# Value products in two runs of five key tiles, convolution taps spread evenly, a query projection one unit later

## The chip, the cores and the metric

One kernel runs on one core of a Trainium2 chip. The metric is the time of one execution on the device, in microseconds (us). The core has five engines, each with a queue of instructions of its own that it works through in order: TensorE (PE; its weight loads are listed as PEld), VectorE (DVE), ScalarE (ACT), GpSimd (POOL), and SyncE (SP), which here issues the transfers between memory and the on-chip buffers. Engines wait for each other only where data or a buffer makes them.

## The reference

Two layers of a hybrid block work on 1024 latent tokens and 256 context tokens. In each layer one input projection feeds three groups: attention, a convolution and a recurrent group. Their outputs are concatenated and go through one output projection, a normalisation and an MLP.

```python
q_l, k_l, v_l = mla_project(cq, ckv, kr, g_qn, w_uq, g_kvn, w_ukv, True)
q_c, k_c, v_c = mla_project(ccq, cckv, ckr, g_qn, w_uq, g_kvn, w_ukv, False)
att = merge_heads(blocked_attend(q_l, concat([k_l, k_c], 2), concat([v_l, v_c], 2)))
conv = conformer_conv(conv_in, conv_w, conv_b, conv_ln_g, conv_ln_b)   # 31 taps, LayerNorm, swish
h_l, h_c = mlstm_bidirectional(...)
y = concat([att, conv, ml], -1) @ w_out
x = layer_norm(ALPHA * x + g1 * y, ln1_g, ln1_b)
```

`attend` is softmax(q k / sqrt(96)) v over 8 heads. Context tokens attend to context tokens only, and are dropped after the first layer.

## The kernel before, in words

The change touches the attention stage, the method `attention`. The stage works through units: one unit is one head and 128 queries against all 1280 keys, which are 10 key tiles of 128. A group `G` is a pair of heads `p` and a block `g` of 256 queries; it has four units (two heads, two query tiles). There are four pairs. In layer 0 a pair has four groups of latent queries and a small one of context queries, whose two units are mixed into those of the fourth (18 units a pair, 72 in all); in the last layer it has four groups (16 units a pair, 64 in all).

The loop over `i` at the end of the method writes out one unit a turn: the score products of unit `i` (`sc`, L77 to L79), the transposes of unit `i - 2` (`et_ps`, copied by ScalarE to `et`), the softmax of unit `i` (L921 on VectorE, L922 on ScalarE), and then what the table `plan` holds for `i`. The table is filled by `at(i, ...)`: `f` is a group's first unit, `qproj(G, e)` makes the queries of its head `e`, `values(G, j0, j1, fin)` multiplies the key tiles `j0` to `j1` of both heads with the values (L868, tile `pv`), and with the last run `norm` follows (two transposes of the softmax sums, L880, two VectorE steps, and a `spill`). A `pv` product uses 64 of TensorE's 128 output columns: head 0 writes partitions 0 to 63, head 1 partitions 64 to 127.

The convolution hides in the same loop. The 31 taps are steps in the list `taps`: half of the channels on VectorE (L444), half on GpSimd (L449, L450). In a unit that stands in `tap_at`, from unit 2 on, one tap is taken. When `taps` is empty, each further unit takes one step of `post`: three empty ones, a transpose `fwd` for each two token tiles, `norm`, three empty ones, and two steps `back` for each two token tiles. That makes 22 steps in layer 0 (10 token tiles) and 19 in the last layer (8). A `back` step is two transposes (L480, `cb_ps`), two activations (L482, L483, `c_v`), a VectorE step (L484) and a `spill`. What is left of `post` runs after the loop:

```python
            if i < nu:
                if i >= 2 and taps:
                    if i in tap_at:
                        taps.pop(0)(pace[i - 1][:2])
                elif not taps and post:
                    post.pop(0)()
        assert not plan
        while post:
            post.pop(0)()
```

`spill` splits a block into a high and a low part on GpSimd (L86, L92, tile `sp`, one buffer for each of the two pools that it is called with) and stores both with SyncE to `cat_d` in memory, from where the output projection reads its input (`xs_hi`, `xs_lo`, L1187).

After the stage its pools are released, that of the convolution (`cv`) and of the query weights (`wq`) among them. `out_proj` then takes pools in the freed space and loads the eight blocks of the output weights (L1195): blocks 0 to 2 through one buffer `wo_raw`, blocks 3 to 7 into `rw`. VectorE splits each (L87, L92) into two tiles `wo`. The products `y_ps` of the first three token tiles run over the blocks in order, 8 blocks x 3 tiles x 2 halves x 3 products.

Pools and dependencies are tracked by a framework, and a scheduler decides in which order the instructions stand in each engine's queue. It starts from the order of the code, and moves instructions by its own estimate of when they can go.

Of the kernel before, what the change touches and what calls it, by code (L numbers as in the profile page):

```python
# [45 lines left out]
class Kern:  # L46
# [752 lines left out]
    def attention(self, l, last, psc, ps, X, wq, A1, A, B, wqk0, taps, post):  # L799
# [26 lines left out]
        def load(p):  # L826
            wr = wq.tile([P, 640], F32, name="wqk_raw", tag="raw", bufs=1)
            t = [wq.tile([P, 640], F32R, name="wqk_s", tag="wqs", bufs=4) for _ in range(2)]
            wqk[p] = self.load_qk(l, p, wr, t)

        def kproj(p, gi):
            wh, wl = wqk[p]
            t0, n = GROUPS[gi]
            pk = ps.tile([P, 512], F32, name="k_ps", tag="aux")[:, :n]
            c = slice(t0, t0 + n)
            ins = self.mm3(pk, wh[:, 512:640], wl[:, 512:640], self.ckn[0][:, c], self.ckn[1][:, c], True, True)
            for e in range(2):
                kh, kl = kb[(2 * p + e) % 3]
                r = slice(64 * e, 64 * e + 64)
                nc.scalar.copy(kh[0:64, c], pk[r])  # L840
                self.last_lo = nc.vector.tensor_tensor(kl[0:64, c], pk[r], kh[0:64, c].bitcast(F32), ALU.subtract)
            return ins

        def qproj(G, e):
            p, g = groups[G]
            wh, wl = wqk[p]
            t0 = g * 256
            pq = ps.tile([P, 256], F32, name="q_ps", tag="aux")
            for j in range(2):
                c = slice(256 * j + 128 * e, 256 * j + 128 * e + 128)  # L850
                self.mm3(pq, wh[:, c], wl[:, c], self.cqn[0][:, j, t0:t0 + 256], self.cqn[1][:, j, t0:t0 + 256], j == 0, j == 1)
            qf = A.tile([P, 256], F32, name="qf", tag="qf")
            nc.vector.tensor_tensor(qf, pq, self.ropeT[:, t0:t0 + 256], ALU.mult)
            qh, ql = qb[(2 * G + e) % 4]
            self.split(qh, ql, qf, "act", "dve")
            qs[G, e] = (qh, ql)

        def pvmm(G, i):
            p, g = groups[G]
            nk = 10 if g < 4 else 2  # L860
            if i >= nk:
                return
            if i == 0:
                pvs[G] = ps.tile([P, 2, 256], F32, name="pv", tag="pv")
            kt = i if last or g not in (2, 4) else (8 + i) % 10
            for e in range(2):
                h = 2 * p + e
                nc.tensor.matmul(pvs[G][64 * e:64 * e + 64, 0], self.V[:, kt, h * 64:h * 64 + 64], ets[G, e][:, kt],  # L868
                                 start=(i == 0), stop=(i == nk - 1))

        def denom(G):

            nc.vector.reciprocal(nms[G][:, 1], nms[G][:, 1])
            nc.scalar.copy(rbs[G].rearrange("p q e d -> p (q e) d"), nms[G][:, 1][:, :, None].to_broadcast([P, 4, 64]))

        def norm(G):
            p, g = groups[G]
            pr = pvs[G][:, 1]
            for q in range(2):
                nc.tensor.transpose(pr[:, q * P:(q + 1) * P], rbs[G][:, q].rearrange("p e d -> p (e d)"), self.ident)  # L880
            rsb = B.tile([P, 256], F32, name="rsb", tag="rsb", bufs=1)
            nc.vector.tensor_copy(rsb, pr)
            nc.vector.tensor_tensor(rsb, pvs[G][:, 0], rsb, ALU.mult)
            self.spill(A1, p, 2 * g, rsb)
# [69 lines left out]
        units, plan, tap_at = [], {}, set()  # L954

        def at(i, *acts):
            plan.setdefault(i, []).extend(acts)

        def values(G, j0, j1, fin):
            for j in range(j0, j1):  # L960
                pvmm(G, j)
            if fin:
                norm(G)

        for G, (p, g) in enumerate(groups):
            if g == 4:
                continue
            f = len(units)
            if G:
                at(f - 3, lambda G=G: qproj(G, 0))  # L970
                at(f - 2, lambda G=G: qproj(G, 1))
            if g < 3 or last:
                units += [(G, *x) for x in four]
                tap_at |= {f, f + 1, f + 2}
                at(f + 6, lambda G=G: denom(G))
                for k, (j0, j1) in enumerate(((0, 3), (3, 5), (5, 8), (8, 10))):
                    at(f + 6 + k, lambda G=G, j0=j0, j1=j1: values(G, j0, j1, j1 == 10))
            else:
                units += [(G, 0, 0), (G, 0, 1), (G + 1, 0, None), (G, 1, 0), (G, 1, 1), (G + 1, 1, None)]
                tap_at |= {f, f + 1, f + 3, f + 4}  # L980
                at(f - 1, lambda G=G: qproj(G + 1, 0))
                at(f + 2, lambda G=G: qproj(G + 1, 1))
                at(f + 6, lambda G=G: denom(G))
                at(f + 7, lambda G=G: values(G, 0, 10, True))
                at(f + 8, lambda G=G: denom(G + 1))
                at(f + 9, lambda G=G: values(G + 1, 0, 2, True))
            if g == 0 and p + 1 < HEADS // 2:
                at(f, lambda p=p: load(p + 1))
            if g == 3 and p + 1 < HEADS // 2:
                for gi, k in enumerate((2, 2, 3) if last else (3, 4, 5)):  # L990
                    at(f + k, lambda p=p, gi=gi: kproj(p + 1, gi))
# [1297 lines left out]
```

## Time and profile before

| what | value |
|---|---|
| three runs | 3201.37, 3201.81, 3207.8 us; median 3201.81 us |
| the profiled execution | 3209.91 us, its span 3208.1 us |
| TensorE busy, share of the span | 3050.6 us, 95% |
| VectorE, ScalarE, GpSimd busy | 2069.2, 1391.5, 1314.7 us (64%, 43%, 41%) |
| attention stage, first to last value product | layer 0: 387.9 to about 730 us; layer 1: to 2376.8 us |

The profile is of one execution. Busy time is the union of an engine's instructions; matmuls overlap in the array, and an instruction's own time is longer than the distance to the next. An idle time is put down to what ended it.

### The profile page before, as it was taken

Reading aid. Unit: us, or ns where it says so; the run is one execution under the profiler, and the core shown is the slowest. Engines: PE = TensorE matmul, PEld = TensorE weight load, DVE = VectorE, ACT = ScalarE, POOL = GpSimd, SP = SyncE. Lnnn points to the kernel's source line nnn. Section 1 sums busy time; section 2 is a strip of 40 time slices with the busy share of each in tenths; the row PEclk is TensorE's granted clock in tenths of the full one; section 3 lists DMA queues with packets and bytes.
Section 4 is the critical chain, followed back from the end, with each engine's and each line's share of the span. In section 5 each row is a group of like instructions: output and inputs, shape, how many; then the busy total and the mean of one; then the engine's idle time right before and its main releaser. Section 6 shows DMA issues by size and latency. Waiting matters only on the chain. (4 is left out here: it accounts for less than half of the span.)

```text
span 3208.1 us, 50116 instructions
## 1 busy us (share of the span) xinstructions
PE 3050.6 (95%) x19354; PEld 2542.6 (79%) x19354; DVE 2069.2 (64%) x3562; ACT 1391.5 (43%) x2736; POOL 1314.7 (41%) x1134
## 2 busy tenths in 40 slices
PE   7999999999899999999999999999999899999987
PEld 4779777777699999777777879777767899977765
DVE  3164678655854444778898265677648755578897
ACT  2142566672443333433334332566644433353332
POOL 0021488210321111477771531477111422268885
PEclk9999999999999999999999999999999899999998
DMA  7521100026433333544423432100053333342322
GB/s 261 199 67 49 47 18 15 16 72 233 166 121 105 106 105 108 168 157 133 157 87 134 159 81 59 47 14 14 15 202 132 105 104 104 105 145 98 103 95 99
DMA packets 213583, 337.23 MB, mean 105 GB/s; under 512 B 13760, under 2 KB 134592, under 8 KB 211296
## 3 DMA queue, kind: packets, MB, share of 16 engines
q1 hardware_dynamic: 213344, 334.03, 32.0%
q8 instruction: 152, 2.49, 0.3%
q14 instruction: 87, 0.71, 0.1%
HBM read 253.05 MB, written 80.92 MB: 104 GB/s over the span
## 5 line engine op out<-in xcount | busy, mean ns | idle before, releaser
L1379 PE MATMUL c_ps<-xs_hi,wm 128*128 128x256 f32 x2560 | 512.4, 288 | 12.7 <-DVE rw L2185 9.5
L1379 PEld LDWEIGHTS c_ps<-xs_hi,wm 128*128 128x128 f32 x2560 | 422.3, 195 | 21.7 <-DVE rw L2185 10.0
L1379 PE MATMUL o_ps<-xs_hi,xs_lo 128*128 128x512 f32 x1458 | 379.3, 398 | 27.3 <-DVE acc L2185 20.3
L1379 PE MATMUL c_ps<-xs_lo,wm 128*128 128x256 f32 x1280 | 366.8, 287 | 3.2 <-DVE xs_lo L2185 3.2
L1379 PEld LDWEIGHTS o_ps<-xs_hi,xs_lo 128*128 128x128 f32 x1458 | 271.9, 190 | 97.9 <-DVE acc L2185 25.9
L2185 DVE TENSOR_TENSOR acc<-o_ps,acc 128x512 f32<-128x512 f32 x405 | 270.9, 682 | 63.1 <-PE o_ps L1379 61.8
L1379 PEld LDWEIGHTS c_ps<-xs_lo,wm 128*128 128x128 f32 x1280 | 249.5, 195 | 3.9 <-DVE xs_lo L2185 3.6
L84 ACT COPY et<-et_ps 128x512 f32<-128x512 f32 (+1 forms) x392 | 198.7, 515 | 95.5 <-PE et_ps L947 90.5
L1379 PE MATMUL c_ps<-bx,wm 128*128 128x256 f32 x1536 | 230.3, 289 | 4.1 <-ACT bx L2185 2.3
L1379 PEld LDWEIGHTS c_ps<-bx,wm 128*128 128x128 f32 x1536 | 206.6, 196 | 7.5 <-POOL bx L2185 3.0
L1379 PE MATMUL o_ps<-wm,xs_lo 128*128 128x512 f32 x783 | 206.8, 396 | 5.3 <-DVE acc L2185 5.3
L92 DVE TENSOR_TENSOR wm<-rw,wm 128x512 fp32r<-128x512 f32 x175 | 140.1, 802 | 109.8 <-ACT wm L84 104.7
L84 ACT CAST wm<-rw 128x512 fp32r<-128x512 f32 x175 | 108.4, 621 | 229.9 <-PE c_ps L1379 175.1
L1409 POOL TENSOR_TENSOR w_s<-w_s,rw 128x512 f32<-128x512 f32 x30 | 40.3, 1343 | 380.8 <-DVE wm L92 380.8
L868 PE MATMUL pv<-et,V 128*64 128x256 f32 x1312 | 194.6, 391 | 0.0
L1379 PEld LDWEIGHTS o_ps<-wm,xs_lo 128*128 128x128 f32 x783 | 146.3, 189 | 40.7 <-DVE acc L2185 7.2
L450 POOL TENSOR_TENSOR conv_acc<-conv_acc,tap 128x656 f32<-128x656 f32 x120 | 170.4, 1420 | 9.7
L921 DVE TENSOR_SCALAR_CACHE_REDUCE E<-sc 128x1280 f32<-128x1280 f32 x91 | 135.5, 1489 | 60.2 <-PE sc L79 59.4
L1443 ACT ACTIVATE hb<-c_ps,fm 128x256 f32<-128x256 f32 x240 | 112.7, 474 | 129.3 <-PE c_ps L1379 119.9
L77 PE MATMUL sc<-kq 128*128 128x512 f32 (+1 forms) x400 | 166.0, 415 | 2.1 <-DVE E L921 1.2
L2185 POOL TENSOR_TENSOR xs_hi<-rw,xs_hi 128x512 fp32r<-128x512 f32 x94 | 138.8, 1492 | 57.2 <-ACT xs_hi L2185 56.7
L947 PE MATMUL et_ps<-ident,E 128*128 128x128 f32 x910 | 149.4, 276 | 1.8 <-ACT et L84 1.2
(504 smaller groups left out, 7785.3 us busy)
## 6 DMA issues: line engine op xcount, KB each, us to landing
rw<-in_w_mlp SPq DMA_DIRECT2D x126, 512.0 KB
hb<-h_d SPq DMA_DIRECT2D x72, 512.0 KB
h_d<-hb SPq DMA_DIRECT2D x64, 512.0 KB
wada<-in_w_ada SPq DMA_DIRECT2D x96, 256.0 KB
cat_d<-sp SPq DMA_DIRECT2D x144, 128.0 KB
wada<-in_w_ada SPq DMA_DIRECT2D x16, 1024.0 KB
w_raw<-in_w_in SPq DMA_DIRECT2D x20, 512.0 KB
xs_hi<-cat_d SPq DMA_DIRECT2D x18, 512.0 KB
```

Source lines behind the costliest of these rows:

```text
L77: mm(ps, lh, rh, start=first, stop=False)
L84: return nc.scalar.copy(out, in_)
L92: return h, e.tensor_tensor(lo, src, hi.bitcast(F32), ALU.subtract)
L450: nc.gpsimd.tensor_tensor(aj[:, c], aj[:, c], m, ALU.add)
L868: nc.tensor.matmul(pvs[G][64 * e:64 * e + 64, 0], self.V[:, kt, h * 64:h * 64 + 64], ets[G, e][:, kt], start=(i == 0), stop=(i == nk - 1))
L921: dve = nc.vector.tensor_scalar(E, s[:, c], -1.0, None, ALU.mult, ALU.min, accum_out=nms[G][:, 0, x:x + 1])
L947: nc.tensor.transpose(pt[:, j], E[:, (i0 + j) * P:(i0 + j + 1) * P], self.ident)
L1379: ins = self.nc.tensor.matmul(ps, x, y, start=first and i == 0, stop=i == len(todo) - 1, skip_group_check=True)
L1409: tt(sums[i], sums[i], a11, ALU.subtract)
L1443: self.nc.scalar.activation(h[:, :, q], b, AF.Identity, bias=f[:, FM_B1 + 2 * i + q % 2:FM_B1 + 2 * i + q % 2 + 1])
L2185: ins = f(*a, **k)
```

## The change

The value products of a group of four units come in two runs of five key tiles, at its units `f + 6` and `f + 8`, and no longer in four runs of three, two, three and two at `f + 6` to `f + 9`. The second query projection of a group comes one unit before the group's first, and no longer two. And where a group took a tap in three of its four units, it now takes one in every other; only the first group of each pair in layer 0, and the first three of each pair in the last layer, keep three.

```diff
             f = len(units)
             if G:
                 at(f - 3, lambda G=G: qproj(G, 0))
-                at(f - 2, lambda G=G: qproj(G, 1))
+                at(f - 1, lambda G=G: qproj(G, 1))
             if g < 3 or last:
                 units += [(G, *x) for x in four]
-                tap_at |= {f, f + 1, f + 2}
+
+                tap_at |= {f, f + 1, f + 2} if g < (3 if last else 1) else {f, f + 2}
                 at(f + 6, lambda G=G: denom(G))
-                for k, (j0, j1) in enumerate(((0, 3), (3, 5), (5, 8), (8, 10))):
-                    at(f + 6 + k, lambda G=G, j0=j0, j1=j1: values(G, j0, j1, j1 == 10))
+                for k, j0, j1 in (6, 0, 5), (8, 5, 10):
+                    at(f + k, lambda G=G, j0=j0, j1=j1: values(G, j0, j1, j1 == 10))
```

The scheduler makes more of it than the diff tells, in the two attention stages and up to the start of the output projections. Three places follow. First, TensorE in layer 0, a run of value products of before; `et_ps` are the transposes of softmax rows, `sc` the scores.

```order
L79 MATMUL sc<-kq 128x256
L947 MATMUL et_ps<-ident,E_3276 128x128 x2
L868 MATMUL pv<-et,V 64x256 x6
L947 MATMUL et_ps<-ident,E_3277 128x128
L77 MATMUL sc<-kq 128x512
```

And such a place in the changed kernel:

```order
L79 MATMUL sc<-kq 128x256
L868 MATMUL pv<-et,V 64x256
L947 MATMUL et_ps<-ident,E_3276 128x128 x2
L868 MATMUL pv<-et,V 64x256 x9
L880 MATMUL pv<-ident,rb 128x128 x2
```

Where three key tiles of both heads stood in one run, five now stand in two: one product alone, then two transposes, then nine. Over both layers there were 172 runs, 72 of them of an odd number of products; now there are 152, 124 of them odd, with 656 products in either.

Second, TensorE where the attention stage of layer 0 ends, before:

```order
L947 MATMUL et_ps<-ident,E_3277 128x128 x10
L868 MATMUL pv<-et,V 64x256
L935 MATMUL et_ps<-ident,krT 128x128 x4
L868 MATMUL pv<-et,V 64x256 x19
L880 MATMUL pv<-ident,rb 128x128 x2
L77 MATMUL y_ps<-wo_6824,xs_hi 128x512
L78 MATMUL y_ps<-wo_6825,xs_hi 128x512
```

The same place after:

```order
L868 MATMUL pv<-et,V 64x256 x15
L880 MATMUL pv<-ident,rb 128x128 x2
L480 MATMUL cb_ps<-ident,zt 128x128 x6
L868 MATMUL pv<-et,V 64x256 x4
L880 MATMUL pv<-ident,rb 128x128 x2
L77 MATMUL y_ps<-wo_6824,xs_hi 128x512 x2
L78 MATMUL y_ps<-wo_6825,xs_hi 128x512
```

Three `back` steps (`cb_ps`, two transposes each) now stand behind the long run of value products. In the last layer two of them stand there, behind a run of twenty.

Third, SyncE at the same place, before (`wo_raw` and `rw` are loads of output weights, `xs_hi` and `xs_lo` of the projection's input, `cat_d` the stores of a spill):

```order
L504 DMA cat_d_96<-sp 128x2x128
L1195 DMA wo_raw<-in_w_out 128x1024 x2
L1187 DMA xs_hi<-cat_d_95 128x1024 x2
L1195 DMA wo_raw<-in_w_out 128x1024
L504 DMA cat_d_95<-sp 128x2x128
L504 DMA cat_d_96<-sp 128x2x128
L1187 DMA xs_hi<-cat_d_95 128x1024 x3
L504 DMA cat_d_95<-sp 128x2x128
```

and after:

```order
L504 DMA cat_d_95<-sp 128x2x128
L504 DMA cat_d_96<-sp 128x2x128
L1188 DMA xs_lo<-cat_d_96 128x1024
L1196 DMA rw<-in_w_out 128x1024
L1196 DMA wo_raw<-in_w_out 128x1024
L1196 DMA rw<-in_w_out 128x1024 x3
L1196 DMA wo_raw<-in_w_out 128x1024
L1196 DMA rw<-in_w_out 128x1024
```

Before, three pairs of stores still came behind the first weight load; now the first weight load stands behind the last of all stores. It is the same in the last layer.

## Rows read from the trace of the kernel before

**Rows 1.** Busy by stretch: us, length, busy PE, PEld, DVE, ACT, POOL (instructions), PEclk, DMA.

```profile
400.00:725.00 325.00, 323.12 (x2152) 238.06 (x2152) 227.26 (x379) 221.00 (x438) 181.23 (x169) 1.00 0.11 33
2075.00:2375.00 300.00, 299.24 (x2003) 220.72 (x2004) 194.16 (x312) 205.65 (x382) 148.55 (x158) 1.00 0.10 32
```

**Rows 2.** Timeline of TensorE in layer 0: start us, us, what, [idle <- what ended it].

```profile
460.81 0.65 PE L868 MATMUL pv<-et,V 128*64 128x256 f32 x4
461.39 0.20 PEld L947 LDWEIGHTS et_ps<-ident,E 128*128 128x128 f32 x2 [0.38 <-issue]
...
705.66 0.65 PE L868 MATMUL pv<-et,V 128*64 128x256 f32 x2
706.23 0.44 PE L947 MATMUL et_ps<-ident,E 128*128 128x128 f32 x2
706.60 1.51 PE L868 MATMUL pv<-et,V 128*64 128x256 f32 x10
708.04 0.39 PE L77 MATMUL q_ps<-cqn,wqk_s 128*128 128x256 f32 x1
...
720.53 1.04 PE L947 MATMUL et_ps<-ident,E 128*128 128x128 f32 x8
```

**Rows 3.** Timeline: a `back` step of layer 0, its first activation and its split.

```profile
655.50 0.56 ACT L482 ACTIVATE c_v<-cb_ps,fm 128x256 f32<-128x256 f32 x1 [0.58 <-PE cb_ps L480]
...
657.56 0.73 POOL L92 TENSOR_TENSOR sp<-c_v,sp 128x256 fp32r<-128x256 f32 x1
```

**Rows 4.** Timeline of GpSimd at the end of layer 0's attention.

```profile
729.38 0.41 POOL L86 TENSOR_SCALAR sp<-rsb 128x256 fp32r<-128x256 f32 x1 [6.32 <-DVE rsb L883]
...
732.64 0.41 POOL L86 TENSOR_SCALAR sp<-rsb 128x256 fp32r<-128x256 f32 x1 [2.04 <-DMA cat_d<-sp]
```

**Rows 5.** Timelines: first weight loads of layer 0, and layer 1's with their splits.

```profile
709.04 6.14 SPq L1195 DMA_DIRECT2D wo_raw<-in_w_out  x2
...
2359.50 0.73 POOL L92 TENSOR_TENSOR sp<-c_v,sp 128x256 fp32r<-128x256 f32 x1
2362.77 0.35 SPq L1195 DMA_DIRECT2D wo_raw<-in_w_out  x1
2366.71 0.69 DVE L87 CAST wo<-wo_raw 128x1024 fp32r<-128x1024 f32 x1 [2.00 <-DMA wo_raw<-in_w_out]
2367.44 1.23 DVE L92 TENSOR_TENSOR wo<-wo_raw,wo 128x1024 fp32r<-128x1024 f32 x1
2368.69 0.33 SPq L1195 DMA_DIRECT2D wo_raw<-in_w_out  x1
```

**Rows 6.** Timelines: normaliser's transposes, and first use of the three tiles, either layer.

```profile
727.80 0.44 PE L880 MATMUL pv<-ident,rb 128*128 128x128 f32 x2
763.42 2.05 DVE L1248 TENSOR_TENSOR rw<-y_ps,g 128x512 f32<-128x512 f32 x3 [7.10 <-PE y_ps L79]
...
2377.09 0.44 PE L880 MATMUL pv<-ident,rb 128*128 128x128 f32 x2
2412.24 2.05 DVE L1248 TENSOR_TENSOR rw<-y_ps,g 128x512 f32<-128x512 f32 x3 [10.80 <-PE y_ps L79]
```

**Rows 7.** Timelines: the five later weights of layer 0, issued and first used.

```profile
737.15 2.96 SPq L1195 DMA_DIRECT2D rw<-in_w_out  x5
743.03 0.69 DVE L87 CAST wo<-rw 128x1024 fp32r<-128x1024 f32 x1 [11.23 <-DMA rw<-in_w_out]
```

**Rows 8.** Timeline of TensorE in layer 0's output projection, behind a wait.

```profile
734.96 0.72 PE L79 MATMUL y_ps<-wo,xs_lo 128*128 128x512 f32 x2 [1.89 <-DMA xs_lo<-cat_d]
...
735.99 0.63 PE L79 MATMUL y_ps<-wo,xs_lo 128*128 128x512 f32 x1
...
738.55 0.63 PE L77 MATMUL y_ps<-wo,xs_hi 128*128 128x512 f32 x1
...
741.46 0.39 PE L77 MATMUL y_ps<-wo,xs_hi 128*128 128x512 f32 x1
741.69 0.39 PE L78 MATMUL y_ps<-wo,xs_hi 128*128 128x512 f32 x1
```

## The prediction

> **What bounds the kernel now.** I read the busy time by stretch first, because the change touches only the two attention stages and the place where each hands over to the output projection. Over most of both stages TensorE is busy 323.12 of 325 us and 299.24 of 300 us at full granted clock, while VectorE, ScalarE and GpSimd are busy at most 70% of the time [rows 1]. So inside attention a TensorE microsecond is a microsecond of the kernel, and work moved on the other engines costs nothing while it stays under that cover. The reader is to see there that only 1.88 + 0.76 = 2.6 us of visible TensorE idle time are left to win. Next I read TensorE's timeline for the price of the value products (`pv`), and then the timelines of ScalarE, GpSimd, SyncE and VectorE around the ends of the stages, because the order of the changed kernel moves transfers there.
>
> **Value products.** Two `pv` records are one product of one head. A run of one product lasts 0.57 us until the next instruction starts (705.66 to 706.23), a run of two 0.58 us (460.81 to 461.39), a run of five 1.44 us (706.60 to 708.04) [rows 2]. From run two to run five are two more pairs, (1.44 - 0.58) / 2 = 0.43 us each. The two heads of a key tile write different halves of the output partitions, and a pair takes what a single one takes: an odd run wastes half a pair. Beside its pairs a run costs 0.58 - 0.43 = 0.15 us when it is left (the next weights wait 0.38 us for no other engine), and at its start the two transposes ahead of it hold TensorE 0.37 us, where two in a long series take 2 x 1.04 / 8 = 0.26 us [rows 2]: 0.11 us, together 0.26 us a run.
>
> Counting the order, before has 172 runs of `pv`, 72 of them odd, which makes (656 + 72) / 2 = 364 pairs; after has 152 runs, 124 odd, 390 pairs. The four runs of 6, 4, 6, 4 that the code asks for mostly stood whole; the two runs of ten mostly become one and nine, since the scheduler lets the first product go ahead of two late transposes. So 26 pairs x 0.43 = +11.2 us, and 20 runs x 0.26 = -5.2 us: **+6.0 us**. Bounds: -5.2 us if the odd halves cost nothing, +11.2 us if the switches are hidden.
>
> The TensorE tiling rule fits in here. The Trainium skill, TensorEngine Tiling (Array Packing), section Key Properties, says that changing the tiling mode, not just the tile, drains the TensorE, and that different tiles run in parallel. The 0.38 us wait agrees with the first; by it alone, 40 fewer changes of mode would make the kernel 5.2 us faster by the row's price, which is the second rival below. The second agrees with the equal times of one and two products, and speaks against runs cut at an odd place.
>
> **Taps and the query projection.** The number of taps (31 a layer), projections, softmaxes and transposes stays. The second projection of a group now comes one unit before the group's first, three before its own scores, with two softmaxes and their transposes between. The even taps change when VectorE and GpSimd work. Both lie under the full TensorE of [rows 1]: 0, and if that cover were gone in places, about the 2.6 us of visible idle either way.
>
> **What the taps push back.** The convolution's `post` steps start after the last tap, one a unit. In layer 0 the last tap moves from unit 44 to 52 of 72, in layer 1 from 42 to 46 of 64. The 22 and 19 steps no longer fit: 3 steps `back` are left after the loop in layer 0 and 2 in layer 1, where before all had run by units 66 and 61. Each is two transposes on TensorE, two activations, one VectorE step, a split on GpSimd and two stores.
>
> This matters because the first three output weights (`wo_raw`) go to space that the convolution gives back. In layer 1 the last split of the convolution ends at 2359.50 + 0.73 = 2360.23, and the first weight load is issued 2.54 us later, at 2362.77, when the stores have read their buffer; in layer 0 the loads began at 709.04, well before the value products ended at 727.80 [rows 5, 6]. So these loads, and their splits on VectorE, now lie under TensorE's work. In the changed order they stand on SyncE's queue behind the last stores of the convolution, in both layers, and behind the last value products. TensorE has nothing else in its order than the output products that need them.
>
> The new path, with 0 at the normaliser's transposes after the long last run of `pv` (727.80 and 2377.09 in before). A `back` step takes 657.56 + 0.73 - 655.50 = 2.8 us from its first activation to the end of its split [rows 3]. GpSimd splits one spill in 1.22 us, and the next split starts 732.64 - 729.38 = 3.26 us after the last, 2.04 us of it a wait until the store has read the single buffer [rows 4]. It takes up the group's own values 729.38 - 727.80 = 1.58 us after 0, and the first step's split, ready by then or soon after, ends at 1.58 + 2 x 1.22 = 4.0. Each later step waits for the buffer, 3.26 us. So the last split ends at 4.0 + 2 x 3.26 = 10.5 us in layer 0 and at 7.3 us in layer 1, and 2.54 us later the first weight can be loaded: 13.1 and 9.8. The three loads share one buffer, so that each waits for the split of the one before: 2368.69 - 2362.77 = 5.92 us a round [rows 5]. The third is split 3 x 5.92 = 17.8 us later, at 30.9 and 27.6. What is left for TensorE then are 12 products of it and 5 x 18 of the five later weights, 102 x 0.23 = 23.5 us [rows 8]: the first three tiles end at 54.4 and 51.1 us. Before, they ended at 763.42 - 727.80 = 35.6 and 2412.24 - 2377.09 = 35.1 us [rows 6]. **+18.8 and +16.0 = +34.8 us.**
>
> Two additions. The loads now share the queues with the five later weights and the transfers of the inputs: five loads together landed 5.9 us after their issue [rows 7], one alone 3.9 us, so a round lasts 0 to 2 us longer, 0 to 12 us over six rounds. VectorE also splits later weights between. I take **+3 us**, since the third round has fewer beside it. And after an idle of 1.89 us in before the products lasted 0.63 instead of 0.39 us from 735.99 to 738.55 and the one that began there, some 3 us of which about 3 x (1 - 0.39 / 0.63) = 1.1 us were lost [rows 8]. Each layer gets three longer pauses, and only the slow stretch after the last is not covered by the next load. I take 1.5 us a layer: **+3 us**, bounds 0 and 8 (1.1 us after each of six pauses, and a little more).
>
> **Sum.** 6.0 + 34.8 + 3 + 3 = +46.8 us. Against the profiled execution's own time of 3209.91 us (span 3208.1 and 1.8 us around it) this is 3256.7. That execution lies 8.1 us over the median of the three runs, 3201.81, with which the result is compared; the change is the same there: 3248.6, taken as **3248 us**. Everything behind starts from these output products, so I see nothing that gives the time back.
>
> **Rivals.**
> - *The weights are partly hidden* (0.08). If in each layer two of the three rounds lay under the value products, as they did before, 2 x 11.8 us of the chain would go: +23, 3225 us. For it: the loads began 19 us ahead of the end in layer 0 [rows 5, 6]. Against it: on SyncE they now stand behind the last stores of the convolution.
> - *Faster, by fewer switches* (0.04). Only the drains count, the odd halves cost nothing, and the three loads find their space before the last `pv` run ends, so that TensorE never waits: 3201.8 - 5.2 = 3196.6 us. It decides if the last stores are read at least 17.8 us, three rounds, before the value products end. For it: before was nearly such a case. Against it: two or three convolution steps stand behind these products on TensorE.
> - *No measurable change* (0.03). The drains saved pay for the odd halves, and the `back` steps left over overlap with the last long run: 3202 us.
> - *Worse* (0.05). Every one of the six rounds lasts 2 us longer (12 instead of 3), all odd halves and no switches count (11.2 instead of 6.0), and the products after each pause are slow (8 instead of 3): 46.8 + 9 + 5.2 + 5 = +66, 3268 us, and more if the inputs' transfers are late too.
> - *As forecast* (0.80), from 3226 (`pv` at -5.2, no contention, no slow products: +29.6, and 5 us less if each layer's chain starts 2.5 us sooner) to 3268 us.
>
> The range 3226 to 3268 holds the forecast's own bounds; the other cases at both ends are the 2 in 10 that it leaves out. About 0.2%, 6 us, is what a measurement of this kernel can tell from no change. Faster by more: 0.04; within: 0.03; slower: 0.93.
>
> **What would show it.** Right: in both layers TensorE idles some 15 us between the last `pv` and the first `y_ps`, waiting for `wo`, with more waits before the second and third weight; the first `wo_raw` issue comes about 2.5 us after the convolution's last split; `pv` has about 150 runs, with a time of 0.57 us for single ones; within attention the two stages differ by less than 10 us. Wrong: `wo_raw` loads that start before the last long `pv` run, or an output projection that ends as long after the last `pv` as before; or VectorE and GpSimd waits within attention that give or take more than 10 us.

## The result, and the profile after

| | before | changed |
|---|---|---|
| median | 3204.45 us (3201.37 to 3207.8, 4 runs) | 3256.85 us (3252.3 to 3260.57, 4 runs) |
| ratio to before | | 1.0158, 95% interval 1.0135 to 1.0180 |
| profiled execution, span | 3209.91, 3208.1 us | 3259.53, 3257.8 us |

The change costs 1.58%, some 51 us; the two profiled spans differ by 49.7 us. I cut both traces at the same places: the first score product of a stage, the normaliser's transposes after the long run of `pv`, and the first use of the output products on VectorE. Of before, [rows 6] has the last two; the first is this row in either layer:

```profile
366.20 0.63 PE L77 MATMUL sc<-kq 128*128 128x512 f32 x1
...
2043.52 0.63 PE L77 MATMUL sc<-kq 128*128 128x512 f32 x1
```

The same places in the changed kernel (timelines of TensorE and VectorE):

```profile
366.51 0.63 PE L77 MATMUL sc<-kq 128*128 128x512 f32 x1
...
732.64 0.44 PE L880 MATMUL pv<-ident,rb 128*128 128x128 f32 x2
789.56 2.05 DVE L1249 TENSOR_TENSOR rw<-y_ps,g 128x512 f32<-128x512 f32 x3 [16.33 <-PE y_ps L79]
...
2066.84 0.63 PE L77 MATMUL sc<-kq 128*128 128x512 f32 x1
...
2409.47 0.44 PE L880 MATMUL pv<-ident,rb 128*128 128x128 f32 x2
...
2463.66 2.05 DVE L1249 TENSOR_TENSOR rw<-y_ps,g 128x512 f32<-128x512 f32 x3 [16.07 <-PE y_ps L79]
```

| stretch | before | changed | difference |
|---|---|---|---|
| attention, layer 0 (score to normaliser) | 361.6 | 366.1 | +4.5 |
| handover, layer 0 (normaliser to first use) | 35.6 | 56.9 | +21.3 |
| attention, layer 1 | 333.6 | 342.6 | +9.1 |
| handover, layer 1 | 35.1 | 54.2 | +19.0 |
| all else, same order in both | | | -4.2 |

So 40.3 us come at the two handovers, 13.6 us within attention; what is left differs between executions of the same instructions.

**The handover.** The reader is to see in the next rows a chain over four engines. TensorE, layer 0, changed kernel:

```profile
732.91 0.60 PE L480 MATMUL cb_ps<-ident,zt 128*128 128x128 f32 x4
...
735.38 0.44 PE L880 MATMUL pv<-ident,rb 128*128 128x128 f32 x2
754.41 1.19 PE L77 MATMUL y_ps<-wo,xs_hi 128*128 128x512 f32 x2 [18.59 <-DVE wo L87]
...
756.11 0.63 PE L79 MATMUL y_ps<-wo,xs_lo 128*128 128x512 f32 x1
...
759.41 0.39 PE L79 MATMUL y_ps<-wo,xs_lo 128*128 128x512 f32 x1
...
761.59 1.65 PE L77 MATMUL y_ps<-wo,xs_hi 128*128 128x512 f32 x6 [0.40 <-DVE wo L87]
...
768.15 1.66 PE L77 MATMUL y_ps<-wo,xs_hi 128*128 128x512 f32 x6 [1.25 <-DVE wo L87]
```

GpSimd, where the last splits of the stage wait for the stores to have read their buffer:

```profile
734.09 0.41 POOL L86 TENSOR_SCALAR sp<-rsb 128x256 fp32r<-128x256 f32 x1 [3.77 <-DVE rsb L883]
...
739.30 0.41 POOL L86 TENSOR_SCALAR sp<-rsb 128x256 fp32r<-128x256 f32 x1 [2.61 <-DMA cat_d<-sp]
...
743.71 0.41 POOL L86 TENSOR_SCALAR sp<-c_v 128x256 fp32r<-128x256 f32 x1 [2.02 <-DMA cat_d<-sp]
744.20 0.72 POOL L92 TENSOR_TENSOR sp<-c_v,sp 128x256 fp32r<-128x256 f32 x1
```

SyncE's queue, with the loads that answer to [rows 5], and VectorE's splits of two of these weights:

```profile
744.14 1.18 SPq L504 DMA_DIRECT2D cat_d<-sp  x2
745.37 0.50 SPq L1188 DMA_DIRECT2D xs_lo<-cat_d  x1
745.96 0.40 SPq L1196 DMA_DIRECT2D rw<-in_w_out  x1
748.14 0.33 SPq L1196 DMA_DIRECT2D wo_raw<-in_w_out  x1
...
755.49 0.33 SPq L1196 DMA_DIRECT2D wo_raw<-in_w_out  x1
...
763.83 0.33 SPq L1196 DMA_DIRECT2D wo_raw<-in_w_out  x1
```

```profile
753.51 0.69 DVE L87 CAST wo<-wo_raw 128x1024 fp32r<-128x1024 f32 x1 [0.63 <-DMA rw<-in_w_out]
...
767.40 0.69 DVE L87 CAST wo<-wo_raw 128x1024 fp32r<-128x1024 f32 x1 [1.73 <-DMA wo_raw<-in_w_out]
```

The last split ends at 744.92, the first weight is issued 3.2 us later (709.04 in before, ahead of the last value products), it is split from 753.51 on, and TensorE, which had nothing else in its order, starts at 754.41 after 18.59 us. (At 753.51 the profile names an `rw` load as what ended the wait; the split reads `wo_raw`.) What SyncE waited for between the `rw` load and this weight is a store of a spill, 1.5 us, by the view of waits (us in total, times, longest):

```profile
SPq L1196 <- DMA cat_d<-sp: 1.6, 2, 1.5
```

Layer 1 has the same picture with a wait of 18.01 us. Behind the pause the products last 0.63 us, then 0.39 from 759.41 on. The granted clock, the column ahead of the last two, was 0.51 from 754.40 to 759.40, about the lower of TensorE's two levels (1.2 GHz), after the 18.59 us in which it had nothing to do; from 759.40 to 761.00 it was 1.00:

```profile
754.40:759.40 5.00, 4.99 (x11) 3.57 (x12) 4.93 (x6) 0.00 (x0) 0.00 (x0) 0.51 0.86 303
```

**Within attention.** The windows that answer to [rows 1] (length, busy PE, PEld, DVE, ACT, POOL, granted clock, DMA):

```profile
400.00:730.00 330.00, 326.35 (x2148) 241.27 (x2148) 217.60 (x372) 218.24 (x431) 174.79 (x162) 1.00 0.08 24
2095.00:2395.00 300.00, 299.99 (x1928) 221.25 (x1926) 184.79 (x303) 196.65 (x366) 134.64 (x151) 1.00 0.06 18
```

TensorE is busy for nearly the same share as before, and takes longer. One place of layer 1 shows a part of the reason, a run of ten that became one and nine:

```profile
2184.39 0.65 PE L868 MATMUL pv<-et,V 128*64 128x256 f32 x2
2184.96 0.44 PE L947 MATMUL et_ps<-ident,krT 128*128 128x128 f32 x2
2185.33 2.37 PE L868 MATMUL pv<-et,V 128*64 128x256 f32 x18
2187.64 0.50 PE L77 MATMUL sc<-kq 128*128 128x512 f32 x1
```

One product takes 0.57 us and nine take 2.31 us, as 0.15 + 0.43 x 5 would be. Summed over all runs, each from its start to the next instruction's, `pv` takes 182.7 us in before (172 runs) and 190.6 us now (152 runs).

### The profile page after: what moved, and what is told of

Same layout as the page of the kernel before. It is cut to its first block, busy times and chain, and to the rows that moved or that the text cites. A ratio compares the mean times of both kernels' runs of the same rounds, so it can differ in the third digit from the quotient of the medians.

```text
span 3257.8 us, 50104 instructions
## 1 busy us (share of the span) xinstructions
PE 3060.9 (94%) x19354; PEld 2550.7 (78%) x19354; DVE 2057.4 (63%) x3562; ACT 1389.9 (43%) x2736; POOL 1302.3 (40%) x1134
## 4 chain that ended last, share of the span: by engine, by line
PE 73%; DVE 12%; issue 4%; DMA 4%; POOL 4%; ACT 3%; SPq 0%; DVEq 0%; POOLq 0%; ACTq 0%
PE c_ps L1380 18%; PE o_ps L1380 12%; PE pv L868 6%; PE et_ps L947 4%; PE cx_ps L1380 3%; PE sc L77 2%; PE sc L78 2%; DVE acc L2186 2%; PE sc L79 2%; PE ada L185 1%; DVE rw L2186 1%; PE o_ps L665 1%; POOL h_s L2186 1%; PE cq_ps L79 1%; PE cq_ps L78 1%
## 5 line engine op out<-in xcount | busy, mean ns | idle before, releaser
L1410 POOL TENSOR_TENSOR w_s<-w_s,rw 128x512 f32<-128x512 f32 x30 | 40.3, 1343 | 380.0 <-DVE wm L92 380.0
L450 POOL TENSOR_TENSOR conv_acc<-conv_acc,tap 128x656 f32<-128x656 f32 x120 | 157.7, 1314 | 10.0
L77 PE MATMUL y_ps<-wo,xs_hi 128*128 128x512 f32 x288 | 112.6, 404 | 42.9 <-DVE wo L87 22.7
```

The lines of the kernel that those rows point to most:

```text
L77: mm(ps, lh, rh, start=first, stop=False)
L450: nc.gpsimd.tensor_tensor(aj[:, c], aj[:, c], m, ALU.add)
```

## The experiments

Unless it is told otherwise an edit is made to the kernel before. The stage times are cut in each kernel's trace as above; a ratio is that to the kernel before on the same chip. A stage time is that of one execution. Of the longer edits (heads apart, whole runs, short copies, pinned pairs) the diff shows the deciding lines alone.

| kernel | ratio, 95% interval | attention 0 | handover 0 | attention 1 | handover 1 |
|---|---|---|---|---|---|
| before | 1 | 361.6 | 35.6 | 333.6 | 35.1 |
| changed | 1.0158, 1.0135 to 1.0180 | 366.1 | 56.9 | 342.6 | 54.2 |
| taps alone | 1.0099, 1.0083 to 1.0115 | 359.3 | 56.5 | 331.4 | 49.1 |
| all but the taps | 1.0052, 1.0035 to 1.0069 | 364.4 | 36.3 | 341.8 | 36.5 |
| two steps a unit | 1.0074, 1.0054 to 1.0093 | 370.2 | 37.5 | 345.3 | 32.3 |
| two raw buffers | 1.0161, 1.0147 to 1.0175 | 365.0 | 53.7 | 342.8 | 49.3 |
| value runs alone | 1.0059, 1.0038 to 1.0081 | 366.8 | 35.9 | 341.4 | 37.5 |
| query alone | 0.9993, 0.9980 to 1.0005 | 366.5 | 35.6 | 327.4 | 33.9 |
| query, last layer | 0.9978, 0.9964 to 0.9992 | 361.4 | 35.5 | 327.2 | 33.3 |
| heads apart | 1.0123, 1.0099 to 1.0147 | 387.1 | 35.3 | 347.6 | 33.4 |
| whole runs | 0.9997, 0.9983 to 1.0011 | 360.8 | 37.0 | 330.7 | 37.0 |
| whole runs, short copies | 0.9969, 0.9956 to 0.9982 | 351.2 | 37.6 | 326.3 | 39.3 |
| before, short copies | 0.9966, 0.9951 to 0.9980 | 351.1 | 37.7 | 328.6 | 33.6 |
| pinned pairs | 1.0077, 1.0060 to 1.0094 | 365.7 | 35.5 | 347.4 | 37.3 |

### What the taps do

**Taps alone.**

```diff
-                tap_at |= {f, f + 1, f + 2}
+                tap_at |= {f, f + 1, f + 2} if g < (3 if last else 1) else {f, f + 2}
```

> The kernel before with the new taps alone. Theory (late output weights): the order has 363 pairs in 168 runs of value products (364 in 172 before), so -0.4 and -1.0 us; in layer 0 six convolution transposes stand behind the long run as in the change, in layer 1 four of them stand just ahead of the last run of 20 (4.6 us earlier than in the change). The handover then costs about +21 us in layer 0 and some +14 us in layer 1, together about +34 us: about 3238 us, with TensorE idle for some 15 us before the first output product in either layer. Rival (the value runs or the query projection are what makes the convolution late): no change within 6 us.

3236.48 us, ratio 1.0099: 32 us, and in the trace +20.9 and +14.0 us at the handovers. TensorE in layer 1, where the steps stand ahead of the last run:

```profile
2385.19 0.60 PE L480 MATMUL cb_ps<-ident,zt 128*128 128x128 f32 x4
2386.42 4.54 PE L868 MATMUL pv<-et,V 128*64 128x256 f32 x40 [0.63 <-DVE rsb L883]
...
2403.71 1.19 PE L77 MATMUL y_ps<-wo,xs_hi 128*128 128x512 f32 x2 [12.39 <-DVE wo L87]
```

The wait is 12.39 us where it was 18.01 in the changed kernel: the run of 4.47 us now hides a part of the chain. Within attention the taps cost nothing (-2.3 and -2.2 us).

**All but the taps** (the changed kernel with that line as before).

> The change without its taps: value products and query projection as changed, taps as before. Order: 389 pairs in 147 runs. Theory: 25 x 0.43 - 25 x 0.26 = +4.3 us, no wait at the handover, about 3208 us; the value products' own time (start to next start) rises by 25 x 0.43 - 25 x 0.15 = +7 us. Rival 1 (only switches count): 3204 - 6.5 = 3198 us, and the value products' own time falls. Rival 2 (the runs make the output weights late, not the taps): 3240 us or more.

3218.24 us, ratio 1.0052. The handovers are those of before within 1.4 us, so that rival 2 falls; rival 1 falls too, since attention is 2.8 and 8.2 us longer. But the 4.3 us of my price are too few: the ratio makes it some 17 us. By ratios this kernel and the last make 0.52% + 0.99% = 1.51% of the 1.58%.

**Two steps a unit** (the changed kernel):

```diff
                 elif not taps and post:
                     post.pop(0)()
+                    if post and i >= nu - 12:
+                        post.pop(0)()
```

> The whole change, but in the last 12 units of a stage two convolution steps are taken a unit, so that none is left after the loop. Order: the weight loads stand on SyncE's queue where they stood before, 390 pairs in 157 runs. Theory (late weights are the loss): the handover is as before, +7.3 us remain of the value products: about 3211 us, 45 us under the change. Rival (the loss lies within attention, the taps slow VectorE or GpSimd there): it stays above 3235 us.

3228.68 us, 18 us more than I had expected. The weights come early again (in layer 0 the first issue stands ahead of the normaliser at 745.70), and the handovers fall by 19.4 and 21.9 us to 37.5 and 32.3:

```profile
731.86 0.35 SPq L1198 DMA_DIRECT2D wo_raw<-in_w_out  x1
```

Attention is 4.1 and 2.7 us longer than in the changed kernel, which I had not expected; that the steps pressed together do this is argued. So the convolution steps left over, which make the weights late, are shown to be the loss at the handover, and the repair is not free. No run moved the weights alone: with two steps a unit the last stores and the loads of the projection's input come earlier too. That these did not hold TensorE is read from the rows of the changed kernel, where each wait shown at the handover ends with `wo`.

**Two raw buffers** (the changed kernel):

```diff
-            raw = W1.tile([P, D], F32, name="wo_raw", tag="raw") if k < 3 else self.rw[:, k - 3]
+            raw = W1.tile([P, D], F32, name="wo_raw", tag="raw", bufs=2) if k < 3 else self.rw[:, k - 3]
```

> The whole change, with two buffers for the first three output weights, so that the second is loaded beside the first and one of the two waits for a split falls away in each layer. The order within attention is that of the change. Theory (the wait before the first output product stays, since it is that for the last stores; behind it the rounds through one buffer set the pace of the first products, partly covered by the slow products after the pause, 36 products in some 10 us): the third weight's products begin 3 to 4 us sooner in each layer, about 7 us in all: 3250 us. Rival 1 (each round counts in full, as in the sum of the prediction): 2 x 6.6 = 13 us, 3243 us. Rival 2 (only the pause before the first product counts): no change, 3257 us.

In the trace the handovers are 3.2 and 4.9 us shorter, together 8 us, as the theory had it. SyncE and TensorE:

```profile
757.81 0.81 SPq L1196 DMA_DIRECT2D wo_raw<-in_w_out  x2
...
764.77 1.19 PE L77 MATMUL y_ps<-wo,xs_hi 128*128 128x512 f32 x2 [19.04 <-DVE wo L87]
```

The pause before the first product stays in layer 0 (19.04 for 18.59 us) and is 16.48 for 18.01 us in layer 1; the short ones behind it go. The whole time does not show it: 3252.12 us, but at a ratio of 1.0161 (1.0158 for the changed kernel) on a chip on which before took 3199.85, as rival 2 has it. Eight us are 0.25%, which the two intervals leave open, so the gain stands on one execution's trace and is not shown in the time. Rival 1, 13 us, falls.

### What the value runs and the query do

**Value runs alone** (the two lines of the diff on `values`).

> The kernel before with the two runs of five key tiles alone. Order: 390 pairs in 157 runs (before 364 in 172), weight loads in their old place. Theory: the value products' own time rises by 26 x 0.43 - 15 x 0.15 = +8.9 us, and TensorE's weight loads for transposes wait longer for ScalarE's copies, since fewer runs fill those waits: some +5 us as in the change without taps; about 3218 us. Rival (the projection's move made those waits): +9 us less 15 x 0.11, about 3211 us.

3223.14 us, ratio 1.0059, and +5.2 and +7.8 us in attention. That is the loss of the kernel without the taps, within the intervals; the value runs make it, and the rival falls. In layer 0 TensorE's weight loads wait 14.1 us for the copies of the transposes, where it is 7.5 in before.

**Query alone** (`at(f - 1, ...)` for the second projection).

> The kernel before with the query projection one unit later, alone. Order: 356 pairs in 156 runs. Theory: own time of the value products -8 x 0.43 - 16 x 0.15 = -5.8 us, and 16 runs fewer to fill waits for ScalarE's copies, +0.3 us each: about 3203 us, no change. Rival 1 (price of a pair and a run alone): -7.6 us, 3197 us. Rival 2 (the later projection is the loss of the change within attention): 3210 us or more.

3200.43 us, no measurable change, but the sum hides two parts: +4.9 us in layer 0, -6.2 in layer 1. In layer 0 the move puts the projection into the unit in which the context group's first one stands, `at(f - 1, ...)` of `qproj(G + 1, 0)`, four times; that this is what costs is argued, not shown. The last layer has no such group:

```diff
-                at(f - 2, lambda G=G: qproj(G, 1))
+                at(f - (1 if last else 2), lambda G=G: qproj(G, 1))
```

> The kernel before with the later query projection in the last layer alone. Order of layer 0 as before; in layer 1 167 pairs in 72 runs (173 in 80). Theory (in layer 0 the later projection meets that of the context group in one unit, four times, and TensorE waits; in the last layer there is no such group and the fewer odd runs are won): attention of layer 1 6 us shorter, layer 0 as before: about 3198 us. Rival (the gain in layer 1 was of one execution): within 3 us of before.

3196.61 us, ratio 0.9978: a little faster than before, by 0.22%, and the gain stands where it was expected (327.2 for 333.6 us in layer 1, layer 0 as before). Six pairs and eight runs fewer are 6 x 0.43 + 8 x 0.15 = 3.8 us of it.

**Heads apart.**

```diff
-            for j in range(j0, j1):
-                pvmm(G, j)
+            for e in range(2):
+                for j in range(j0, j1):
+                    pvmm(G, j, (e,))
```

> The kernel before, with each value run written first for one head, then for the other, so that products that write the same half of the partitions follow each other. Theory (two products pass together only where they write different halves): 656 products in some 536 slots of 0.43 us (one overlap in each of 120 runs) instead of 364: +74 us, about 3280 us; 3330 us where no two overlap. Rival (a product costs half a slot whatever half it writes, and a run a fixed time): within 8 us of before.

3242.31 us, ratio 1.0123, and attention is 39.5 us longer. TensorE, with six products that take 1.45 us in before, and sixteen that would take 0.15 + 8 x 0.43 = 3.6 us:

```profile
450.74 2.00 PE L868 MATMUL pv<-et,V 128*64 128x256 f32 x12
452.67 0.50 PE L77 MATMUL k_ps<-ckn,wqk_s 128*128 128x512 f32 x1
...
466.26 6.31 PE L868 MATMUL pv<-et,V 128*64 128x256 f32 x32
472.51 0.44 PE L880 MATMUL pv<-ident,rb 128*128 128x128 f32 x2
```

They take 1.93 and 6.25 us. Runs of two products, 0.58 us in before, take 1.01 us in 14 of 16 cases. So products that write the same half do not pass together, and the rival falls. That products of different halves do is what the Trainium skill, TensorEngine Tiling (Array Packing), section Key Properties, says of different tiles running in parallel, and the trace agrees (0.57 us for one product, 0.58 for one of each head). My 74 us were too many: most short runs of both heads keep their time (35 of 43 runs of four products take 1.02 us, as in before).

**Whole runs** (all but the taps, and the first product of a run ordered behind the last transpose written ahead of it):

```diff
+                if e == 0 and first:
+                    self.after(ins, self.last_tr)
```

> As the change without its taps, but the first product of each value run is ordered behind the last transpose that the code writes ahead of it, so that the runs of ten stand whole: 333 pairs in 68 runs (before 364 in 172). Theory (0.43 us a pair, 0.26 us a run): -13.3 - 27.0 = -40 us: about 3164 us. Rival (the run that stands whole makes TensorE wait for ScalarE's copies of the transposes, some 0.3 us at each of 60 runs, and the odd halves are all that is won): -13 + 18, within 6 us of before.

3204.22 us, no change: the rival. From start to next start, `pv` with its normaliser falls by 27.4 us (190.5 to 163.1), for 31 x 0.43 + 104 x 0.15 = 28.9 by the count; the transposes rise by 17.2 us (148.1 to 165.3) and the scores by 5.3. TensorE's waits for the copies of the transposes, weight loads and products of both layers, rise from 16.4 to 27.6 us, 11.2 of these 22.5 us. The view of waits, first TensorE's weight loads in layer 0, before, then changed, then whole runs, then its products with whole runs (us in total, times, longest):

```profile
PEld et_ps L947 <- ACT et L84: 7.5, 20, 0.5
```

```profile
PEld et_ps L947 <- ACT et L84: 12.9, 36, 0.4
```

```profile
PEld et_ps L949 <- ACT et L84: 13.1, 32, 1.1
...
PE et_ps L949 <- ACT et L84: 4.5, 13, 0.9
```

And two such waits with whole runs, on ScalarE and on TensorE:

```profile
483.94 0.59 ACT L84 COPY et<-et_ps 128x512 f32<-128x512 f32 x1 [0.97 <-PE et_ps L949]
...
628.25 0.58 ACT L840 CAST kq<-k_ps 64x512 fp32r<-64x512 f32 x1
628.86 0.37 ACT L84 COPY et<-et_ps 128x256 f32<-128x256 f32 x1
```

```profile
483.30 0.60 PE L949 MATMUL et_ps<-ident,E 128*128 128x128 f32 x4
484.58 0.33 PE L949 MATMUL et_ps<-ident,E 128*128 128x128 f32 x1 [0.68 <-ACT et L84]
...
627.98 0.44 PE L949 MATMUL et_ps<-ident,E 128*128 128x128 f32 x2
629.28 1.09 PE L949 MATMUL et_ps<-ident,E 128*128 128x128 f32 x8 [0.87 <-ACT et L84]
```

At the first TensorE waits 0.68 us for a copy that starts at once; at the second 0.87 us for one that has to let a conversion of keys go first on ScalarE. Nothing else stands between the transposes in TensorE's order, since the value products are kept for one run. A single product there wastes half a pair, but it is work for such a time.

**Short copies**, of the whole runs and then of before:

```diff
-                    self.copy("act", et[:, kts[i0]:kts[i0] + m, q * P:(q + 1) * P], pt)
+                    self.copy("act", et[:, kts[i0]:kts[i0] + m, q * P:q * P + 32], pt[:, :, :32])
```

> As the kernel with whole runs and the taps of before, but ScalarE copies a quarter of the columns of each transposed block only (the values are multiplied with what is left, zeros for the most part; a clearing of the buffer is added at the stage's start). Theory (in the whole-run kernel TensorE's weight loads for transposes wait for these copies, and that took back what the runs won): copies shorter by some 0.3 us at some 80 waits, 20 to 30 us under the whole-run kernel, about 3178 us, and the weight loads' wait for copies falls to a third. Rival (the waits belong to the softmax or to the scores): no gain over the whole-run kernel, about 3204 us.

> The kernel before with ScalarE's copies of the transposed blocks cut to a quarter of their columns, as in the whole-run kernel with short copies (the values are multiplied with zeros for the most part). Order: 352 pairs in 152 runs (364 in 172), so -5.2 - 3.0 = -8 us of own time. Theory (in before the value runs already cover the copies): little more than these 8 us, about 3195 us. Rival (short copies shorten any kernel by the 10 us that they gave the whole-run kernel): 3186 us.

3193.83 and 3193.78 us. The whole runs gain 10 us, less than expected, and their weight loads' wait for copies in layer 0 falls from 13.1 to 9.6 us, not to a third. Before gains 11, some 8 of them, by the count of pairs and runs, from the order that the scheduler then finds. With short copies in both, the whole runs are thus still no faster than before (ratios 0.9969 and 0.9966), so that the length of the copies alone is not what took their gain. What else makes TensorE wait, such as a copy's turn on ScalarE, was read in the rows above and not tried by itself.

**Pinned pairs** (the kernel before; a key tile of both heads fixed between the second and third block of transposes):

```diff
+                if j == 2 and vals and len(tp) == 3:
+                    G, j0, j1 = vals[0]
+                    vals[0] = (G, j0 + 1, j1)
+                    for k in range(j0, j0 + 1):
+                        pvmm(G, k, k == j0)
+                    filled = self.last_pv
```

> The kernel before, with the order of each value run pinned: one key tile of both heads (two products) between the second and the third block of transposes, the rest behind the third. Order: 332 pairs in 225 runs (364 in 172). Theory (an odd half is lost, and a run between the transposes covers a wait for ScalarE's copy): -32 x 0.43 + 53 x 0.15 = -5.8 us own time, and shorter waits at the transposes: 6 to 9 us under before, about 3197 us. Rival (each run costs 0.26 us whatever it covers): -13.8 + 13.8 = 0, no change.

3228.65 us, a miss: 0.77% slower. `pv` falls by 4.5 us (190.5 to 186.0), near the 5.8 of the count, but the transposes rise by 9.4 us and the scores by 13.5 (263.1 to 276.6). With nearly no odd run left, 53 runs more and a fixed order cost more than 32 half pairs. The theory's own sign is against it: in layer 0 the weight loads wait 18.0 us for the copies, where it is 7.5 in before. A pair put between the transposes did not cover that wait.

## Why the prediction was right

It gave 3248 us, 3226 to 3268; 3256.85 was measured, and the difference of the spans is 49.7 us for the 46.8 of the sum. The mechanism at the handovers was right. That the sum is so near is in part luck: attention lost 7.6 us more than forecast, and 4.2 us of that were given back by stretches whose order is the same in both kernels.

- **Late output weights** (+34.8, with +3 for contention and +3 for slow products): 40.3 us measured for 40.8. The path was as described: the taps alone bring it, all but the taps don't, and two steps a unit remove it. That the two numbers agree to 0.5 us is luck, since four errors cancel.
    - The first weight was issued 15.5 and 12.3 us after the normaliser, not 13.1 and 9.8: some 5 us more. The last split ended 12.3 and 8.1 us after it instead of 10.5 and 7.3 (two waits for the single split buffer in layer 0 were 2.61 and 2.02 us, near the row's 2.04), and the weight came 3.2 and 4.2 us behind that split instead of 2.54.
    - The three rounds lasted 7.35, 8.34 and 5.5 us in layer 0 instead of 5.92 each, in both layers together 7.4 us more, where I had 3. In layer 0 the first two weights were split 5.4 us after their issue, where the row had 3.9, and the third, with none of the later weights under way, 3.6 us after it. That fits the contention, which no run tried by itself. In the second round VectorE also had a part of another weight's split in between, 1.1 us.
    - The slow products cost nothing on this path, for my 3 us. TensorE idled 18.6 us before the first weight and only 0.4 to 1.3 us before the others, since the slow products and the longer blocks filled the rounds (18 products from 754.41 to 761.03 in 6.6 us, where 18 x 0.23 = 4.1), and it still waited for the next weight behind them.
    - I let the chain end with the last of 102 products, but compared it with the first use on VectorE in [rows 6], which comes 15 products earlier. That is 15 x 0.23 = 3.4 us too much in each layer; behind the third split 20.2 us passed in either, not 23.5.
- **Value runs** (+6.0): their own time rose by 7.9 us, for 8.2 by pairs and the 0.15 at the end of a run. The other part of my price, 20 x 0.11 = 2.2 us saved at the transposes ahead of a run, is not to be seen; the waits there grew instead, in layer 0 from 7.5 to 12.9 us. Attention as a whole got 13.6 us longer, and by 13.0 us with the value runs alone, beyond the bounds of -5.2 and +11.2 that I gave the term. It is the term which was mis-sized: I gave a run a price and did not ask how the order around it changes the waits.
- **Taps and query projection at nothing** within attention: right in the sum (the query alone 0.9993, the taps -4.5 us), wrong as two parts for the query, +4.9 and -6.2 us.
- **The rivals.** "Faster, by fewer switches" falls with the heads apart and with the whole runs: a run's end has the price that the row gave, 0.15 us, and the odd halves cost theirs. Weights partly hidden did not come about in the changed kernel. "No measurable change" and "worse" fall with the time.

## What to carry to other kernels

A step list that fills up idle slots has an end, and the end has a successor: spreading the filler evenly let its last pieces slip behind the last full-size work, the next stage's loads waited behind their stores, and that stage began to deliver some 20 us later at each of two places. Two products that share the array by halves are priced by the pair, so count odd runs before making runs longer; but the order around the runs counts as much: of 27 us won on the array by whole runs most came back at the transposes and scores, half of it as waits for copies. That a run between transposes covers such a wait is argued; the kernel that pinned a pair there waited more. Where the busy share is 99%, look at the waits of the weight loads too.

## What the runs showed of the hardware that was not expected

The stretch before the attention stage has the same TensorE work in all these kernels but the two with short copies, and took from 364.8 us (whole runs, mean granted clock 0.97) to 380.1 us (value runs alone, 0.93) in the other 12 profiles. The windows of before and of the value runs alone (columns as in [rows 1]):

```profile
120.00:180.00 60.00, 53.91 (x389) 41.78 (x383) 24.36 (x87) 15.87 (x43) 16.72 (x23) 1.00 0.40 118
180.00:240.00 60.00, 57.37 (x370) 49.32 (x367) 39.01 (x70) 27.09 (x85) 8.92 (x6) 0.89 0.21 52
```

```profile
120.00:180.00 60.00, 55.66 (x392) 43.35 (x391) 26.17 (x92) 16.80 (x47) 16.95 (x24) 0.97 0.42 116
180.00:240.00 60.00, 58.35 (x299) 50.59 (x297) 35.13 (x59) 18.83 (x59) 5.03 (x4) 0.69 0.16 40
```

TensorE is about as busy in both, but its granted clock is 0.89 in the one and 0.69 in the other from 180 to 240 us, so it was for a longer part of these at the lower of its two levels, 1.2 GHz, and got through 299 instead of 370 matmuls. Single executions differ by up to 15 us in this stretch, a third of the effect measured here, which is why stages were compared and not only whole times.
